# An mLSTM stage on one core: TensorE's order written out with a second branch's products handed out between, and the state weights' exponentials moved

## The chip, the cores and the metric

The kernel runs on one core of a Trainium2 chip. The metric is the device time of one execution in microseconds (us). A core has TensorE (PE: matmuls, with its weight loads shown as PEld), VectorE (DVE), ScalarE (ACT), GpSimd (POOL) and SyncE (SP), which issues most DMAs. Each engine takes its own instructions in order and waits on semaphores for the others.

## What is computed

One decoder layer for 512 tokens of width 1024 in float32: an mLSTM branch and a sliding-window attention branch read the same normalised input, their outputs are gated, merged and projected; then come an MLP, a gated embedding and a last norm. The change touches the mLSTM and the merge:

```
def step(carry, chunk):                       # per head, chunk after chunk
    C, n, m = carry
    b = cumsum(fc); log_d = where(causal, b[t] - b[s] + ic[s], -inf); inter = b + m
    m_t = maximum(inter, max(log_d))
    scores = (q @ k.T) * exp(log_d - m_t)
    w_inter = exp(inter - m_t)
    num = w_inter * (C @ q) + scores @ v
    den = w_inter * (n @ q) + sum(scores)
    h = num / maximum(abs(den), exp(-m_t))
    w = exp(b_last - b + ic - m_new); decay = exp(b_last + m - m_new)
    C_new = decay * C + (w * v) @ k.T;  n_new = decay * n + w @ k
...
y_a = sigmoid(o_ml) * rmsnorm(h) * g
merged = sigmoid(g_a) * (y_a @ w_branch_a) + sigmoid(g_b) * (y_b @ w_branch_b)
```

`y_b` is the output of the attention branch. There are 4 mLSTM heads with keys of width 128 and values of width 256; the kernel uses chunks of 128 tokens, so a sequence has 4 chunks (`NT`) and a head 3 states that are needed.

## The kernel before, in words

Every large product is done in float32 split into two parts (a high part `wh`, made by a cast on ScalarE, and a rest `wl`, by a subtraction on VectorE), three matmuls for each pair of tiles: a 128x128 weight against 512 columns. A projection of one 128-row tile of the output is thus 8 x 3 = 24 matmuls (24 "products"), accumulated in one bank. `load_w` loads a weight tile and splits it; there are four buffers each for the raw tile, the high part and the rest.

Accumulation banks: two of tag `g` (`psg`, one bank each), two of tag `t` (`pst`, one bank each) and two of tag `a` (`psa`, two banks each). Activations of 512 columns (`act_f`, `act_r`) come from one pool of 36 buffers. Two buffers of tag `pT` hold, in the mLSTM stage, pairs of gates read back from DRAM (`gl`). Four buffers of tag `vs` hold the weighted keys `kw`, four of tag `lm` the values.

A tile framework orders the instructions when the kernel is built: a planner goes by program order as the priority and by durations of its own, puts each instruction in as soon as its inputs and a buffer are ready in its plan, and adds the waits. Inside a block `tc.manual_schedule(engines=...)`, the named engines keep the program's order. `tc.issue_after(x)` puts all instructions of its block that run on the engine of `x` behind `x` on that engine.

The stages that matter here:

- First phase (0 to about 60 us), all engines but POOL in manual order: norm, first projections, the projection for the output gates `o` (`o_open` makes the products, `o_close` returns a function that applies the sigmoid, line 264, and stores the gate in DRAM through POOL's queue), and the scans of the mLSTM's forget and input gates on 4 partitions. `mst` is the running maximum; `pk` collects what is transposed later into `gc`: rows 0 to 3 hold exp(-mst), 32 to 35 the exponents `gg`, 64 to 67 the exponents of the states' weights, 96 to 99 those of the inter-chunk weights. The gates' sigmoids are put behind `em_last`, the last exponential of the phase. The rows 96 to 99 go to DRAM as `rid`.
- Value projections, branch gates (`gbd`, `gad` in DRAM), then the sliding-window attention (212 to 324 us) with TensorE in manual order: there the products of other projections are handed out by a generator, `more(n)` emitting the next `n`.
- The mLSTM stage, where the planner orders everything. Per head `h`: `ml_weights` loads the rows `pr` and `pi` (broadcast `rid`), transposes three key chunks (L914) and makes the score products (L916) in one `psa` tile, splits the weighted keys `kw` (L143, L144), forms the decay matrix with exponentials of `dg` (L924, L925), and scales the queries (L928); `ml_state` makes three state products and folds them up (L942, L946); `ml_out` makes the output of four chunks in `pst` banks, copies it to `hs` (L959), takes the denominators (L960 to L965) and sums squares (L968); `ml_norm` scales it. `branch_b(i)` is the projection of `y_b` (24 products), multiplied with a branch gate (`gb`, L986); there are eight. `ya_of(h)` transposes a head's output (L998), multiplies it with the output gate (`sy`, L999) and splits it into `ya`. Then eight projections of `ya` (`w_a`) follow.

Of the kernel before, what the change touches and what calls it, by code (L numbers as in the profile page):

```python
# [23 lines left out]
NH = 4  # L24
# [12 lines left out]
def block_kernel(  # L37
# [49 lines left out]
    def nm(s):  # L87
        n_names[0] += 1
        return f"{s}_{n_names[0]}"


    def ps_g():
        return pp.tile([P, 512], F32, tag="g", bufs=2, name=nm("psg"))

    def ps_t():
        return pp.tile([P, 512], F32, tag="t", bufs=2, name=nm("pst"))
# [9 lines left out]
    def act_f(n="f"):  # L106
        return ap.tile([P, 512], F32, tag="act", bufs=NACT, name=nm(n))
# [28 lines left out]
    def split(dst, src, scale=None):  # L136

        if scale is None:
            done = A.copy(dst[0], src)  # L139
            V.tensor_sub(dst[1], src, r32(dst[0]))  # L140
            return done.ins
        else:
            A.activation(dst[0], src, AF.Copy, scale=scale)  # L143
            V.scalar_tensor_tensor(dst[1], src, scale, r32(dst[0]), ALU.mult, ALU.subtract)  # L144
# [7 lines left out]
    def load_w(src, n, dims, raw=None):  # L152

        if raw is None:
            raw = load_raw(src, n)
        parts = [wp.tile([P, 1024], F32R, tag=t, bufs=WB, name=nm(t))[:, :n] for t in ("wh", "wl")]
        split(parts, raw[:, :n])
        return [q.rearrange("p (k c) -> p k c", k=dims) for q in parts]
# [7 lines left out]
    def chain(ps, ops, first, last, parts=False):  # L166
        for i, (l, r) in enumerate(ops):
            last_mm[0] = T.matmul(ps, l, r, start=first and i == 0, stop=last and i == len(ops) - 1, skip_group_check=parts)  # L168
# [13 lines left out]
    def mm_T(ps, w, acts, first=True, last=True):  # L182

        ops = []
        for k in range(len(acts)):
            ops += pairs([q[:, k, :] for q in w], acts[k])
        chain(ps, ops, first, last)
# [120 lines left out]
    with tc.manual_schedule(engines={ENG.PE, ENG.Activation, ENG.DVE, ENG.SP}):  # L308
# [181 lines left out]
        G.memset(pk, 0.0)  # L490
        mst = act_f("mst")[:4, :]
        V.tensor_tensor_scan(mst, lf, ig, 0.0, ALU.add, ALU.max)
        fl = act_f("fl")[:4, :]
        for c in range(NT):
            V.tensor_tensor_scan(fl[:, c * P : (c + 1) * P], lf[:, c * P : (c + 1) * P], zeros4, 0.0, ALU.add, ALU.add)
# [5 lines left out]
        ends = lambda t: chunks(t)[:, :, P - 1 :].broadcast_to([4, 3, P])  # L501
        V.tensor_tensor(chunks(pk[64:68, :]), chunks(gg), ends(rr), ALU.add)
        V.tensor_tensor(chunks(pk[96:100, :]), chunks(rr[:, P:]), ends(mst), ALU.add)
        A.activation(pk[:4, :], mst, AF.Exp, scale=-1.0)
        em_last = A.activation(pk[64:100, : 3 * P], pk[64:100, : 3 * P], AF.Exp).ins
        V.tensor_copy(pk[32:36, :], gg)
        for i in (3, 4):
            gates.append(o_close(i, o_open(i, hT, ow[i])))
# [206 lines left out]
    def gate_of(put, i):  # L715

        if i % 2 == 0:
            loaded[0] = sp.tile([P, 2, 512], F32, tag="pT", bufs=2, name=nm("gl"))
            nc.sync.dma_start(out=loaded[0], in_=put[i // 2])
        return loaded[0][:, i % 2, :]  # L720

    gbd = gate_proj(w_gb)
    gad = gate_proj(w_ga)
# [159 lines left out]
    def h_of(h, t):  # L883
        return hs[h][t // 2][:, (t % 2) * DV : (t % 2 + 1) * DV]

    def ml_weights(h):
        pr = sp.tile([P, 512], F32, tag="pr", bufs=2, name=nm("pr"))
        nc.sync.dma_start(out=pr, in_=rrd[h : h + 1, :].broadcast_to([P, 512]))
        pi = act_f("pi")[:, : 3 * P]
        nc.sync.dma_start(out=pi, in_=rid[h : h + 1, :].broadcast_to([P, 3 * P]))  # L890
        dg = act_f("dg")
        V.tensor_tensor(
            dg.rearrange("p (t j) -> p t j", t=NT),
            pr.rearrange("p (t j) -> p t j", t=NT),
            tri.unsqueeze(1).broadcast_to([P, NT, P]),
            ALU.add,
        )
        if h < 2:
            room = bp.tile([P, KT, 512], F32R, tag="big", bufs=2, name=nm("wT"))
            wT = [room[:, k, :] for k in range(2)]  # L900
            qw = [room[:, k, : 3 * P] for k in range(2, 4)]
            rest = room[:, 4:, :].rearrange("p k c -> p (k c)")
            cs = [[rest[:, (2 * c + j) * (DV + 2) : (2 * c + j + 1) * (DV + 2)] for j in range(2)] for c in range(3)]
        else:
            wT, qw = act_hl("wT"), [t[:, : 3 * P] for t in act_hl("qw")]
            cs = None
        vhl = [head_values() for _ in range(2)]
        for s in range(NT):
            split([v[:, s, :] for v in vhl], vm[s][:, h, :])
        both = ps_a()  # L910
        kt, psc = both[:, 512:], both[:, :512]
        block = lambda t, s: t[:, s * P : (s + 1) * P]
        for s in range(3):
            T.transpose(block(kt, s), block(qk[4 + h], s), ident)  # L914
        for s in range(NT):
            T.matmul(block(psc, s), block(qk[4 + h], s), block(qk[h], s), start=True, stop=True)  # L916
        kw = []
        for s in range(3):
            t = sp.tile([P, 2 * P], F32R, tag="vs", bufs=4, name=nm("kw"))
            kw.append([t[:, :P], t[:, P:]])  # L920
            split(kw[s], block(kt, s), gc[:, 2 * NT + s, h : h + 1])
        dm = act_f("dm")
        for s in range(NT):
            A.activation(block(dm, s), block(dg, s), AF.Exp, bias=gc[:, s, h : h + 1])  # L924
        V.tensor_mul(dm, psc, dm)  # L925
        split(wT, dm)
        qt = act_f("qt")[:, : 3 * P]
        V.tensor_mul(qt, qk[h][:, P:], pi)  # L928
        split(qw, qt)
        wts[h] = wT, qw, cs, kw, vhl, pi  # L930

    def ml_state(h):
        wT, qw, cs, kw, vhl, pi = wts[h]
        if cs is None:
            t = [sp.tile([P, 2 * (DV + 2)], F32R, tag="cs", bufs=3, name=nm("cs")) for _ in range(3)]
            cs = [[c[:, : DV + 2], c[:, DV + 2 :]] for c in t]
        two = ps_a()
        ps = [t[:, : DV + 2] for t in (two[:, :512], two[:, 512:], ps_t())]
        for s in range(3):
            chain(ps[s], pairs(kw[s], [v[:, s, :] for v in vhl]), True, True)  # L940
        state = act_f("st")[:, : DV + 2]
        A.copy(state, ps[0])  # L942
        split(cs[0], state)
        for s in range(1, 3):
            new = act_f("st")[:, : DV + 2]
            V.scalar_tensor_tensor(new, state, pi[:, s * P - 1 : s * P], ps[s], ALU.mult, ALU.add)  # L946
            state = new
            split(cs[s], state)
        wts[h] = wT, qw, cs, vhl

    def ml_out(h):
        wT, qw, cs, vhl = wts.pop(h)
        for t in range(NT):
            pn = ps_t()
            ops = pairs([w[:, t * P : (t + 1) * P] for w in wT], [v[:, t, :] for v in vhl])
            if t:
                ops += pairs([q[:, (t - 1) * P : t * P] for q in qw], cs[t - 1])
            chain(pn[:, : DV + 2], ops, True, True)
            A.copy(h_of(h, t), pn[:, :DV])  # L959
            V.tensor_copy(hd[:, h, t : t + 1], pn[:, DV : DV + 1])  # L960
        den = small("den", NT, 2)
        V.scalar_tensor_tensor(den, hd[:, h, :], -1.0, hd[:, h, :], ALU.mult, ALU.max)
        V.tensor_max(den, den, gc[:, NT : 2 * NT, h])
        rd = small("rd", NT, 3)
        V.reciprocal(rd, den)  # L965
        jk = act_f("jk")
        for t in range(NT):
            A.activation(jk[:, :DV], h_of(h, t), AF.Square, scale=rd[:, t : t + 1], accum_out=hss[:, h, t : t + 1])  # L968
        return rd
# [9 lines left out]

    t2 = [None] * 8  # L980

    def branch_b(i):
        ps = ps_g()
        mm_T(ps, load_w(w_b[i], KT * P, KT), yb)
        t2[i] = act_f("gb")
        V.tensor_mul(t2[i], ps, gate_of(gbd, i))  # L986


    ya = []

    def ya_of(h):
        if not ya:
            ya.extend(big_hl("ya")[1])
        for i in (2 * h, 2 * h + 1):
            sg = act_f("sy")
            pt = ps_t()
            for t in range(NT):
                T.transpose(pt[:, t * P : (t + 1) * P], h_of(h, t)[:, (i % 2) * P : (i % 2 + 1) * P], ident)  # L998
            V.scalar_tensor_tensor(sg, pt, gml[:, i : i + 1], gate_of(god, i), ALU.mult, ALU.mult)  # L999
            split(ya[i], sg)  # L1000

    ml_weights(0)
    ml_state(0)
    rds = []
    for h in range(NH):
        branch_b(2 * h)
        if h + 1 < NH:
            ml_weights(h + 1)
        if h < 2:
            ml_state(h + 1)  # L1010
        rds.append(ml_out(h))
        if h == 2:
            ml_state(h + 1)
        branch_b(2 * h + 1)
        if h == 1:
            ml_norm([0, 1], rds)
        elif h > 1:
            ml_norm([h], rds[h:])
            ya_of(h - 2)
    ya_of(2)  # L1020
    ya_of(3)


    mg = []
# [403 lines left out]
```

## Time and profile before

| | |
|---|---|
| median of 3 runs | 887.67 us (886.52 to 888.81) |
| the profiled execution | 886.76 us, span from first to last instruction 884.4 us |
| TensorE | busy 870.4 us, 98% of the span |
| VectorE, ScalarE | busy 655.2 us (74%), 452.1 us (51%) |
| granted TensorE clock | 0.998 on the mean |
| mLSTM stage, 324.1 to 404.4 us | VectorE busy 63.69 us, ScalarE 57.20 us |

How to read the lines of the profile. A group reads: line, engine, operation, output tile <- input tiles, shape, count, busy us, mean ns of one, idle time of the engine before them and what ended it. A wait reads: engine, tile and line that waited <- what it waited for: us in total, times, longest. A row of the timeline reads: start, duration, engine, line, operation, tiles, shape, count, and in brackets the idle time before it. A row of a stretch reads: from:to, us, then the busy time of PE, PEld, DVE, ACT (and POOL) with the number of instructions, the granted clock, the share of DMA time and GB/s. Where instructions were picked by tile or line, such a row counts only those. Ends of matmuls are modelled, so a busy TensorE may still lose time.

### The profile page before, as it was taken

The page shows a single profiled execution, that of the slowest core. Times are in us where ns is not written, and L with a number is a line of the kernel's source. Part 1 is how long each engine was busy: PE and PEld are TensorE (multiplying, and loading weights), DVE is VectorE, ACT ScalarE, POOL GpSimd, SP SyncE. Part 2 cuts the span into 40 slices and gives each one's busy share as a digit, 9 for nine tenths or more (in the row PEclk, how much of TensorE's full clock was granted, in tenths as well). Part 3 has the DMA queues.
Part 4 walks back from the last instruction along what each step waited for, and adds up shares of the span by engine and source line. Part 5 has one row for each costly group of instructions (what it writes and reads, how often), then busy time and mean ns, then how long its engine had stood idle before and what let it go on. Part 6 is the DMA issues. An engine that isn't in the chain of part 4 may idle for free.

```text
span 884.4 us, 11952 instructions
## 1 busy us (share of the span) xinstructions
PE 870.4 (98%) x4588; PEld 731.9 (83%) x4588; DVE 655.2 (74%) x1057; ACT 452.1 (51%) x753; POOL 13.1 (1%) x36
## 2 busy tenths in 40 slices
PE   9999999999999999999999999999999999999996
PEld 8878899998877877878888888888888888888886
DVE  5998787864887888678534679767957885798556
ACT  6564444454666677764323645335434533444844
POOL 1010000000000000000000000000000000000000
PEclk9999999999999999999999999999999999999999
DMA  8651324453121133336352611620352054102402
GB/s 337 214 203 58 122 96 144 152 172 130 49 72 59 61 129 113 104 104 206 123 186 85 225 48 61 201 96 24 120 176 85 1 190 143 49 24 76 138 1 96
DMA packets 31289, 103.37 MB, mean 117 GB/s; under 512 B 4344, under 2 KB 5372, under 8 KB 31232
## 3 DMA queue, kind: packets, MB, share of 16 engines
q1 hardware_dynamic: 29232, 96.04, 32.0%
q0 software_dynamic: 1856, 6.31, 2.0%
q8 instruction: 36, 0.59, 0.3%
q10 hardware_dynamic: 144, 0.26, 0.1%
q14 instruction: 21, 0.17, 0.1%
HBM read 94.19 MB, written 8.40 MB: 116 GB/s over the span
## 4 chain that ended last, share of the span: by engine, by line
PE 89%; DVE 2%; ACT 1%; issue 0%; ACTq 0%; DVEq 0%
PE psg L168 42%; PE psp L168 23%; PE psa L168 9%; PE psg L844 8%; PE pst L819 2%; PE psa L772 1%; PE psa L806 1%; PE pst L168 1%; PE psp L1058 1%; PE psa L916 0%; DVE prod L1262 0%; PE pst L998 0%; DVE it L1283 0%; ACT sgp L1269 0%; ACT z L1297 0%
## 5 line engine op out<-in xcount | busy, mean ns | idle before, releaser
L139 ACT CAST wh<-wr 128x1024 fp32r<-128x1024 f32 x128 | 134.3, 1051 | 195.0 <-PE psg L168 69.2
L140 DVE TENSOR_TENSOR wl<-wr,wh 128x1024 fp32r<-128x1024 f32 x128 | 155.9, 1221 | 89.5 <-ACT wh L139 89.5
L168 PE MATMUL psg<-x,wh 128*128 128x512 f32 x512 | 158.3, 390 | 0.0
L168 PE MATMUL psp<-wh,uf 128*128 128x512 f32 x448 | 139.1, 390 | 0.0
L168 PEld LDWEIGHTS psg<-x,wh 128*128 128x128 f32 x512 | 96.1, 188 | 19.8
L168 PE MATMUL psg<-x,wl 128*128 128x512 f32 x256 | 99.7, 389 | 0.0
L168 PEld LDWEIGHTS psp<-wh,uf 128*128 128x128 f32 x448 | 84.1, 188 | 17.3
L168 PE MATMUL psp<-wl,uf 128*128 128x512 f32 x224 | 87.3, 390 | 0.0
L139 ACT CAST wh<-wd 128x1024 fp32r<-128x1024 f32 x44 | 46.3, 1055 | 57.7 <-PE psp L168 26.0
L844 PE MATMUL psg<-h,wh 128*128 128x512 f32 x192 | 62.4, 400 | 0.0
L140 DVE TENSOR_TENSOR wl<-wd,wh 128x1024 fp32r<-128x1024 f32 x44 | 53.5, 1220 | 4.4 <-ACT wh L139 4.1
L168 PEld LDWEIGHTS psg<-x,wl 128*128 128x128 f32 x256 | 48.1, 188 | 9.9
L168 PE MATMUL psa<-h,wh 128*128 128x256 f32 (+1 forms) x240 | 50.2, 306 | 1.3 <-ACT sgo L264 1.3
L168 PEld LDWEIGHTS psp<-wl,uf 128*128 128x128 f32 x224 | 42.1, 188 | 8.7
L140 DVE TENSOR_TENSOR uf<-F,uf 128x1792 fp32r<-128x1792 f32 (+2 forms) x20 | 33.0, 1651 | 21.8 <-ACT uf L139 21.8
L168 PEld LDWEIGHTS psa<-h,wh 128*128 128x128 f32 x240 | 38.8, 191 | 4.3 <-ACT sgo L264 1.7
L844 PEld LDWEIGHTS psg<-h,wh 128*128 128x128 f32 x192 | 35.4, 188 | 8.2 <-issue 0.4
L168 PE MATMUL psg<-yb,wh 128*128 128x512 f32 x128 | 41.4, 396 | 0.6 <-DVE gb L986 0.6
L139 ACT CAST uf<-F 128x1792 fp32r<-128x1792 f32 (+2 forms) x20 | 28.0, 1398 | 26.3 <-DVE F L1134 26.2
L1120 DVE SCALAR_TENSOR_TENSOR rt<-psg,rB 128x512 f32<-128x512 f32 x32 | 22.1, 689 | 25.6 <-PE psg L168 25.6
L168 PE MATMUL psg<-ya,wh 128*128 128x512 f32 x128 | 40.5, 395 | 0.0
L791 ACT ACTIVATE lm<-lm,nmx 128x256 f32<-128x256 f32 (+1 forms) x64 | 30.0, 470 | 17.2 <-DVE nmx L784 15.6
(329 smaller groups left out, 1747.3 us busy)
## 6 DMA issues: line engine op xcount, KB each, us to landing
wr<-in_w_up SPq DMA_DIRECT2D x32, 512.0 KB, 3.3
wd<-in_w_down SPq DMA_DIRECT2D x24, 512.0 KB, 3.4
wr<-in_w_o SPq DMA_DIRECT2D x8, 512.0 KB, 6.9
gd<-gr POOLq DMA_DIRECT2D x8, 512.0 KB, 3.0
wr<-in_w_qsw SPq DMA_DIRECT2D x8, 512.0 KB, 3.6
wr<-in_w_qkml SPq DMA_DIRECT2D x8, 512.0 KB, 3.8
wr<-in_w_b SPq DMA_DIRECT2D x8, 512.0 KB, 3.3
gl<-gd SPq DMA_DIRECT2D x8, 512.0 KB, 3.4
```

Of the source, the lines that this page charges most:

```text
L139: done = A.copy(dst[0], src)
L140: V.tensor_sub(dst[1], src, r32(dst[0]))
L168: last_mm[0] = T.matmul(ps, l, r, start=first and i == 0, stop=last and i == len(ops) - 1, skip_group_check=parts)
L772: T.matmul(o, q[x][HALF[ab], n * P : (n + 1) * P], keys[kp][y][HALF[ab], k0 : k0 + 256], start=i == 0, stop=i == 2)
L791: A.activation(lm3[:, g, :], lm3[:, g, :], AF.Exp, bias=nmx[:, g : g + 1], accum_out=sm[:, g : g + 1])
L806: T.transpose(pt[:, c : c + P], lm3[:, g, j * P : (j + 1) * P], ident)
L819: T.matmul(o[HALF[ab], m * 256 : (m + 1) * 256], vs[n + m + 1 - nk + j][:, c : c + 64], pTs[m][:, j * 512 + ab * 256 : j * 512 + (ab + 1) ...
L844: T.matmul(ps, l, r, start=k == 0 and j == 0, stop=k == KT - 1 and j == 2)
L1058: T.transpose(ps[:, m * P : (m + 1) * P], xk[m][:, k * P : (k + 1) * P], ident)
L1120: V.scalar_tensor_tensor(a, ps, 0.0, rB, ALU.max, ALU.mult)
```

## The change

Three things are changed. In the first phase the exponential of `-mst` moves right behind the scan that makes `mst` and becomes the one that the gates' sigmoids are put behind; the second exponential of the phase, over 36 partitions of `pk`, is gone. In its place, the mLSTM stage applies an exponential to 12 columns of `gc` once, and one to `pi` in each `ml_weights`. The whole stage runs with TensorE in manual order: the eight projections of branch b become a generator from which `more(n)` takes products between the parts of the heads, `ya_of` becomes `ya_tile` for one of eight tiles, and two groups of products are handed out inside each `ml_out`. Gates in use are kept by source, so that branch gates and output gates can be in use side by side.

```diff
+        em_last = A.activation(pk[:4, :], mst, AF.Exp, scale=-1.0).ins     # behind the scan of mst
...
-        A.activation(pk[:4, :], mst, AF.Exp, scale=-1.0)
-        em_last = A.activation(pk[64:100, : 3 * P], pk[64:100, : 3 * P], AF.Exp).ins
...
         if i % 2 == 0:
-            loaded[0] = sp.tile([P, 2, 512], F32, tag="pT", bufs=2, name=nm("gl"))
-            nc.sync.dma_start(out=loaded[0], in_=put[i // 2])
-        return loaded[0][:, i % 2, :]
+            loaded[id(put)] = sp.tile([P, 2, 512], F32, tag="pT", bufs=2, name=nm("gl"))
+            nc.sync.dma_start(out=loaded[id(put)], in_=put[i // 2])
+        return loaded[id(put)][:, i % 2, :]
...
         nc.sync.dma_start(out=pi, in_=rid[h : h + 1, :].broadcast_to([P, 3 * P]))
+        A.activation(pi, pi, AF.Exp)
...
             chain(pn[:, : DV + 2], ops, True, True)
+            if t in (1, 2):
+                more(7 - 2 * t)
...
-    def branch_b(i):
-        ps = ps_g()
-        mm_T(ps, load_w(w_b[i], KT * P, KT), yb)
+    def b_done(i, ps):
         t2[i] = act_f("gb")
         V.tensor_mul(t2[i], ps, gate_of(gbd, i))
...
-    ml_weights(0)
-    ml_state(0)
     rds = []
-    for h in range(NH):
-        branch_b(2 * h)
-        if h + 1 < NH:
-            ml_weights(h + 1)
-        if h < 2:
-            ml_state(h + 1)
-        rds.append(ml_out(h))
-        if h == 2:
-            ml_state(h + 1)
-        branch_b(2 * h + 1)
-        if h == 1:
-            ml_norm([0, 1], rds)
-        elif h > 1:
-            ml_norm([h], rds[h:])
-            ya_of(h - 2)
-    ya_of(2)
-    ya_of(3)
+    A.activation(gc[:, 2 * NT :, :], gc[:, 2 * NT :, :], AF.Exp)
...
+    def branches():
+        for i in range(8):
+            w = load_w(w_b[i], KT * P, KT)
+            ps = ps_g()
+            for k in range(KT):
+                for j, (l, r) in enumerate(pairs([t[:, k, :] for t in w], yb[k])):
+                    T.matmul(ps, l, r, start=k == 0 and j == 0, stop=k == KT - 1 and j == 2)
+                    yield
+            b_done(i, ps)
+        yield
+
+    fill = branches()
+
+    with tc.manual_schedule(engines={mybir.EngineType.PE}):
+        more(24)
+        ml_weights(0)
+        ml_weights(1)
+        more(24)
+        ml_state(0)
+        ml_state(1)
+        more(20)
+        rds.append(ml_out(0))
+        ml_weights(2)
+        more(17)
+        rds.append(ml_out(1))
+        ml_state(2)
+        ml_weights(3)
+        norm_of([0, 1])
+        more(17)
+        rds.append(ml_out(2))
+        ml_state(3)
+        norm_of([2])
+        for i in range(4):
+            more(4)
+            ya_tile(i)
+        rds.append(ml_out(3))
+        norm_of([3])
+        more(21)
+        ya_tile(4)
+        more(5)
+        ya_tile(5)
+        more(15)
+        ya_tile(6)
+        for _ in fill:
+            pass
+        ya_tile(7)
```

More of the change, by code (lines that the diff above doesn't have):

```diff
@@ L989, in block_kernel, with ya_tile @@
     ya = []
-    def ya_of(h):
+    def ya_tile(i):
+        h = i // 2
         if not ya:
             ya.extend(big_hl("ya")[1])
[L994 to L1000, printed above, removed]
-    ml_weights(0)
@@ L1003, in block_kernel @@
-    ml_state(0)
-    rds = []
-    for h in range(NH):
-        branch_b(2 * h)
-        if h + 1 < NH:
-            ml_weights(h + 1)
-        if h < 2:
-            ml_state(h + 1)
-        rds.append(ml_out(h))
-        if h == 2:
-            ml_state(h + 1)
-        branch_b(2 * h + 1)
-        if h == 1:
-            ml_norm([0, 1], rds)
-        elif h > 1:
-            ml_norm([h], rds[h:])
-            ya_of(h - 2)
-    ya_of(2)
-    ya_of(3)
+        sg = act_f("sy")
+        pt = ps_t()
@@ new lines, in ya_tile, with norm_of @@
+        for t in range(NT):
+            T.transpose(pt[:, t * P : (t + 1) * P], h_of(h, t)[:, (i % 2) * P : (i % 2 + 1) * P], ident)
+        V.scalar_tensor_tensor(sg, pt, gml[:, i : i + 1], gate_of(god, i), ALU.mult, ALU.mult)
+        split(ya[i], sg)
+    rds = []
+    A.activation(gc[:, 2 * NT :, :], gc[:, 2 * NT :, :], AF.Exp)
+    def norm_of(heads):
+        ml_norm(heads, [rds[h] for h in heads])
+    def branches():
[8 more added lines that the diff above has]
+        yield
```

## The prediction

> **What bounds the kernel now.** I read the page's busy times first, then TensorE's waits, then the timeline around the one wait of the early phase, and last the mLSTM stage (324 to 404 us) alone.
>
> ```profile
> PE 870.4 (98%) x4588; PEld 731.9 (83%) x4588; DVE 655.2 (74%) x1057; ACT 452.1 (51%) x753; POOL 13.1 (1%) x36
> PE pst L998 <- DVE st L946: 1.4, 1, 1.4
> PE psa L168 <- ACT sgo L264: 1.3, 1, 1.3
> ```
>
> TensorE bounds it, and the waits listed for it are short; these are the longest, the first in the mLSTM stage, the second in the early phase. A matmul's end is modelled, though, so short stalls hide in "busy". For the stage I therefore compare the time elapsed with the work done at the undisturbed pace. First the counts: the 512-wide products into `psg`; all matmuls of line 168; then the transposes of L998, the score matmuls of L916 and the transposes of L914.
>
> ```profile
> 324.10:404.40 80.30, 56.67 (x221) 39.40 (x221) 7.58 (x11) 0.00 (x0) 1.00 0.38 128
> 324.10:404.40 80.30, 71.07 (x341) 54.63 (x341) 1.00 0.38 128
> 324.10:404.40 80.30, 4.83 (x32) 3.92 (x32) 1.00 0.38 128
> 324.10:404.40 80.30, 4.23 (x32) 3.88 (x32) 1.00 0.38 128
> 324.10:404.40 80.30, 1.96 (x12) 1.53 (x12) 1.00 0.38 128
> ```
>
> Then the pace, from stretches of the chain of waits in which TensorE ran on without a stop (start, us, what, count):
>
> ```profile
> 347.27 1.43 PE pst L168 x12
> 337.63 0.89 PE psa L916 x8
> 373.93 7.30 PE psg L168 x32
> 395.46 0.88 PE pst L998 x8
> ```
>
> So a product costs 7.30/32 = 0.228 us, a 258-wide matmul 0.119, a score matmul or transpose 0.11. The work is 221 x 0.228 + (341 - 221) x 0.119 + 76 x 0.11 = 50.4 + 14.3 + 8.4 = 73.1 us in 80.3 us: **7.2 us are lost in the stage**. The waits of the weight loads say where:
>
> ```profile
> PEld psa L168 <- ACT kw L143: 2.1, 5, 0.7
> PEld pst L998 <- DVE st L946: 1.8, 1, 1.8
> PEld psa L168 <- DVE kw L144: 1.1, 3, 0.6
> PEld psg L168 <- DVE gb L986: 1.0, 2, 0.5
> ```
>
> The state products come up before their weighted keys `kw` are split (339 to 341.5 and 350 to 354 us), and at 384.5 us the gated output's transposes wait for a bank that the state's update has not read yet. All three are matters of order, none of total load: VectorE is busy 63.7 and ScalarE 57.2 of these 80.3 us.
>
> **The change part by part.**
>
> *1. Exponential of `mst` early, the second one (L505) out of the first phase.* TensorE and ScalarE around the early wait:
>
> ```profile
> 56.69 0.61 PE L168 MATMUL psa<-h,wh 128*128 128x512 f32 x2
> 57.14 0.39 PE L168 MATMUL psa<-h,wl 128*128 128x512 f32 x1
> 58.83 0.73 PE L168 MATMUL psa<-h,wh 128*128 128x512 f32 x2 [1.30 <-ACT sgo L264]
> 50.58 0.63 ACT L504 ACTIVATE pk<-mst 4x512 f32<-4x512 f32 x1 [2.31 <-DVE mst L492]
> 51.90 1.06 ACT L139 CAST wh<-wr 128x1024 fp32r<-128x1024 f32 x1 [0.69 <-PE psa L168]
> 54.78 0.52 ACT L505 ACTIVATE pk<-pk 36x384 f32<-36x384 f32 x1 [1.83 <-DVE pk L503]
> 55.32 1.28 ACT L264 ACT_TABLE_LOAD   x1
> 56.62 1.67 ACT L264 ACTIVATE sgo<-sgo 128x512 f32<-128x512 f32 x3
> 58.20 0.57 ACT L264 ACTIVATE sgo<-psa 128x512 f32<-128x512 f32 x1
> ```
>
> The gates' sigmoids are tied behind the last exponential, which waits for VectorE until 54.78. TensorE's next output projection waits for the fourth sigmoid (58.77). With the exponential of `mst` (done at 51.21) as the last one, table load, three sigmoids, the cast of 51.90 and the fourth sigmoid take 1.28 + 1.67 + 1.06 + 0.57 = 4.6 us, to about 55.8, ahead of TensorE's 57.4. The gap from 57.14 to 58.83 is 1.69 instead of the usual 0.23: **-1.46 us** (none at worst, if the planner puts the sigmoids later). The work up to 324 us has nothing that would hold this back: the DMA of `rid` on POOL leaves a little earlier, and the next weights are cast ahead.
>
> The three small state weights now go through a 12-column exponential, traced before the stage but ready at 71 us, so the planner may place it between two sigmoids, at the price of two table loads, 2 x 1.28 us. ScalarE waits for TensorE there:
>
> ```profile
> 69.83 1.05 ACT L139 CAST wh<-wr 128x1024 fp32r<-128x1024 f32 x1 [3.33 <-PE psg L168]
> 75.74 1.05 ACT L139 CAST wh<-wr 128x1024 fp32r<-128x1024 f32 x1 [4.36 <-PE psg L168]
> ```
>
> 4.36 us of idle time covers 2.6: I cost it at nothing; without that cover it would be at most 2.6. The Trainium skill ("ScalarE: Activation LUTs", What ACT_TABLE_LOAD costs) adds a drain of about 1.38 us to each load, 2.66 in all; by it the two switches would need 5.3 us and overrun the gap by 1. The trace disagrees: the sigmoid at 56.62 starts 0.02 us after its load ends.
>
> *2. Exponential of `pi` (128x384) in each `ml_weights`.* ScalarE does a 384-wide cast in this time:
>
> ```profile
> L139 ACT CAST qw<-qt 128x384 fp32r<-128x384 f32 x2 | 1.0, 514 | 3.1 <-DVE qt L928 3.1
> 325.12 0.42 SPq L890 DMA_DIRECT2D pi<-rid  x1
> DMA to landing us min/median/max: 3.4/3.8/6.4
> 332.26 1.28 ACT L924 ACT_TABLE_LOAD   x1
> 328.31 3.69 DVE L756 SCALAR_TENSOR_TENSOR acc<-acc,sg 128x512 f32<-128x512 f32 x6
> ```
>
> 4 x 0.51 = 2.1 us on ScalarE, off the path. Behind the first one queue the exponentials of the decay; it waits for `pi` to land, 331.5 at the latest (325.12 + 6.4), before the table load has ended (333.54). So no new wait.
>
> *3. TensorE in program order, products of branch b in between.* The ideal is that all 7.2 us go. Counting on from 324.1 in the new order: 24 products to 329.6; keys and scores of heads 0 and 1 (2 x 11 x 0.11 = 2.4) to 332.0; 24 products to 337.5; state 0 (9 x 0.119) to 338.5; then state 1. Two places are late next.
>
> *State 1.* The three splits `kw` of a head use four buffers in all, so the second and third of head 1 wait until state 0 has read the first two of head 0, and state 1 needs the bank in which head 1's keys and scores lie.
>
> ```profile
> L143 ACT ACTIVATE kw<-psa,gc 128x128 fp32r<-128x128 f32 x12 | 4.3, 359 | 1.4 <-PE psa L916 1.2
> L144 DVE SCALAR_TENSOR_TENSOR kw<-psa,gc,kw 128x128 fp32r<-128x128 f32 x12 | 4.2, 346 | 1.1 <-ACT kw L143 1.1
> 324.00:332.00 8.00, 8.00 (x43) 6.59 (x42) 7.96 (x15) 7.05 (x13) 0.00 (x0) 1.00 0.65 221
> 332.00:340.00 8.00, 7.72 (x43) 6.21 (x42) 6.94 (x15) 6.95 (x16) 0.00 (x0) 1.00 0.37 123
> ```
>
> The second product group of state 0 ends at 338.2 (6 x 0.119); split on ScalarE 0.36, on VectorE 0.35, handover 0.2: 339.1 against 338.5, a stall of at least 0.6. VectorE and ScalarE are nearly full in these 16 us (VectorE gets free of the silu only at 332.0), so up to 2.5. I take **+1.5**.
>
> *The gates of the first four `ya` tiles.* The tag `pT` has two buffers. When the `ya` tiles come, one holds the branch gates 4 and 5 until product 144 is done, which stands behind them in the order (at 142). So the output gates 2 and 3 load into the other buffer only after `ya` tile 1 is multiplied, and the two `pst` banks stay taken until tiles 2 and 3 are multiplied, while head 3's output needs them.
>
> ```profile
> DMA to landing us min/median/max: 3.1/3.7/5.5
> L999 DVE SCALAR_TENSOR_TENSOR sy<-pst,gml,gl 128x512 f32<-128x512 f32 x7 | 5.0, 745 | 0.0
> ```
>
> After tile 1's transposes: multiply 0.85, load 3.5, multiply 0.85 = 5.2 us; TensorE has 8 products and 8 transposes meanwhile, 2.7. Stall 2.5, and 0.1 for the restart: **+2.6** (2.1 with the fastest load; 4.0 with a queue ahead on VectorE).
>
> *Restarts and small waits.* The 58.83 row shows two matmuls in 0.73 where others take 0.61: 0.12 a restart. In each head's output 5 products (1.1 us) cover the release of the first bank, which a 1.22 us split ahead on VectorE can overrun. I take **+0.8** (0.3 to 1.5).
>
> All else has cover: each state's chain (a copy, two updates, three splits) gets 16 to 20 products and more before its head's output (3.6 to 4.6 us), and the last `ya` tile is due 23 products later in branch a's first tile.
>
> The sum: -1.46 - 7.2 + 1.5 + 2.6 + 0.8 = **-3.8 us**. The profiled execution took 886.76 us (span 884.4, 2.4 around it), 0.9 below the median of 887.67; against the median, 887.67 - 3.8 = 883.9. With the low ends of the three unknowns (0.6 + 2.1 + 0.3 = 3.0 for 4.9) it is 882.0, and up to 885.0 I count as this case.
>
> **The rivals.**
>
> *A, the new waits are as long as the old.* State 1 stalls 2.5, the gates 4.0, the rest 1.5: 8.0 against 7.2. Only the early phase is left: -0.7, 887.0. For it speaks the full VectorE from 324 to 340; against it that VectorE has 16.6 us free in the stage.
>
> *B, slower: the activation buffers run out at the `ya` tiles.* Of 36, then live: `yb` 16, heads 6, gated products 5, `wT` and `qw` of head 3 4, states 3, `pi` 1 = 35. With one left, each tile waits until the one before is multiplied and split.
>
> ```profile
> L139 ACT CAST ya<-sy 128x512 fp32r<-128x512 f32 x7 | 4.2, 612 | 3.3 <-DVE sy L999 3.2
> L140 DVE TENSOR_TENSOR ya<-sy,ya 128x512 fp32r<-128x512 f32 x6 | 4.0, 682 | 0.0
> ```
>
> 0.75 + 0.61 + 0.68 and queues make 3 us a tile: from the end of state 3, tile 0 at 4.5 (when the state's chain gives a buffer back, an estimate), then 7.5, 11.9 (gate load) and 14.9, and head 3's output stalls 9.9 instead of 2.6. +7.3: 891.2. It decides if no buffer of the state chain is back when tile 1 comes; against it, the three states and `pi` come free as soon as that chain is split. A stall this long bears on the clock too: every window above shows 1.00 granted. The Trainium skill ("TensorE: Matmul & The Clock Gate", HAM oscillation) says that an idle gap above about 3.4 us drops the clock to half; by it B would lose some 1.7 us more (an estimate from that page), and the forecast's 2.6 us nothing. No run here shows such a gap.
>
> *C, the gate wait does not come*, because the second gate load finds a buffer early: -3.8 - 2.6 = -6.4, 881.3. Against it stands the order of the products in the code.
>
> *D, the early edit does nothing*, since the planner places the sigmoids as late as before: 885.4.
>
> **How the numbers follow.** Forecast 0.40, A 0.22, B 0.14, C 0.17, D 0.07. What a measurement of this kernel can tell from no change is about 0.3%, 2.7 us. Faster by more: forecast and C, 0.57; within: A and D, 0.29; slower: B, 0.14. The range goes from C with some of its unknowns at their low ends, 880.5, over A to part of the way to B, 889.0.
>
> **What would show it.** Part 1: no wait of `psa` on L264, and the sigmoid table loaded near 52 us. Part 3: no `pst` L998 wait on L946, no `kw` waits near 351; instead a wait of state 1 on `kw` or `dm` near 337 and one of head 3's first output on the multiply of `ya` tile 2, some 45 us later. The products and transposes keep their pace. The prediction is wrong if ScalarE's or VectorE's order, made by a planner with its own durations, puts a late-needed step ahead of `kw`, or if the stalls move to places not named here.

## The result: 16 us slower, and the profile after

The changed kernel takes 903.67 us (median of 4 runs, 903.28 to 903.88) against 888.11 for the kernel before beside it: a ratio of 1.0177 [1.0160, 1.0195]. The forecast was 883.9. The profiled execution has a span of 901.3 us (before 884.4) at a mean granted clock of 0.987.

In the changed kernel L1014 are the products of branch b, L961 and L962 the copies of an output chunk (`hs` on ScalarE, `hd` on VectorE; both must be done before its bank is free), L925 the multiply of the scores with the decay, L999 the multiply of a `ya` tile. TensorE's waits:

```profile
PE pst L168 <- DVE hd L962: 8.4, 2, 4.4
PE psa L168 <- DVE dm L925: 3.5, 1, 3.5
PE pst L168 <- DVE sy L999: 2.6, 1, 2.6
PE psg L168 <- DVE ya L140: 0.7, 1, 0.7
```

Five waits, all for VectorE: at 337 us (state 1), at 360 and 377 (third chunk of the outputs of heads 1 and 2), at 393 (head 3's output) and at 418. Between the starts of the matmuls around them 3.7, 4.2, 4.5, 2.8 and 1.0 us are missing, 16.2 in all. The stage's products, up to the 220th, in the form of the row of before:

```profile
323.00:421.20 98.20, 59.24 (x220) 42.43 (x221) 7.71 (x11) 0.00 (x0) 0.90 0.36 113
```

By the prediction's pace the same work needs 220 x 0.228 + 120 x 0.119 + 76 x 0.11 = 72.8 us: 25.4 us are lost where 7.2 were before. The 16.2 us of standing still explain two thirds. The rest is in the granted clock, which was 1.00 throughout the stage before. It changes only at the ends of stretches of 3.41 us (last section). Such stretches around the first two waits and around the one at 393 (PE busy, PEld, DVE, ACT, POOL, then the clock):

```profile
335.71:339.13 3.42, 2.01 (x14) 1.62 (x12) 2.52 (x7) 3.19 (x9) 0.00 (x0) 1.00 0.52 143
339.13:342.54 3.41, 1.31 (x10) 1.34 (x11) 3.41 (x7) 1.68 (x4) 0.00 (x0) 1.00 0.36 113
342.54:345.95 3.41, 3.41 (x9) 2.64 (x9) 3.31 (x9) 2.02 (x6) 0.00 (x0) 0.50 0.12 46
345.95:349.37 3.42, 3.42 (x19) 2.92 (x19) 0.59 (x2) 0.37 (x2) 0.00 (x0) 1.00 0.44 153
359.61:363.02 3.41, 0.82 (x4) 0.35 (x2) 2.49 (x4) 1.57 (x2) 0.00 (x0) 1.00 0.00 0
363.02:366.43 3.41, 1.92 (x8) 1.86 (x9) 1.43 (x5) 1.31 (x4) 0.00 (x0) 0.50 0.64 178
366.43:369.85 3.42, 3.42 (x16) 3.23 (x15) 1.59 (x7) 1.82 (x6) 0.00 (x0) 0.50 0.50 187
393.74:397.15 3.41, 1.34 (x9) 1.13 (x10) 2.66 (x6) 1.33 (x3) 0.00 (x0) 1.00 0.16 65
397.15:400.57 3.42, 3.42 (x14) 2.94 (x13) 2.60 (x5) 1.60 (x3) 0.00 (x0) 0.50 0.61 184
```

Behind the first wait (from 342.54) TensorE is busy, at half clock: 9 matmuls in 3.41 us where 15 products would fit. Six such slow stretches (342.5, 363.0 and 366.4, 380.1 and 383.5, 397.2; two behind each of the waits of 4.2 and 4.5 us) make 20.5 us; TensorE is busy for 17.0 of them, and up to half of that, 8.5 us, is lost. With the restarts behind the waits that makes up the other 9 us.

The first phase did what was forecast. The sigmoid table loads at 51.48 instead of 55.32, no matmul waits for L264, and branch b starts at 323.0 instead of 324.1:

```profile
50.84 0.63 ACT L493 ACTIVATE pk<-mst 4x512 f32<-4x512 f32 x1 [2.31 <-DVE mst L492]
51.48 1.28 ACT L264 ACT_TABLE_LOAD   x1
...
70.05 1.28 ACT L1003 ACT_TABLE_LOAD   x1
71.48 0.21 ACT L1003 ACTIVATE gc<-gc 128x12 f32<-128x12 f32 x1 [0.16 <-DVE gc L587]
74.43 1.05 ACT L139 CAST wh<-wr 128x1024 fp32r<-128x1024 f32 x1 [2.73 <-PE psg L168]
75.50 1.28 ACT L264 ACT_TABLE_LOAD   x1
```

The 12-column exponential does fall between two sigmoids with two table loads, and idle time of ScalarE covers them, as costed.

**What ends the long waits.** The wait at 360 us, on TensorE, ScalarE and VectorE in turn:

```profile
359.82 0.61 PE L1014 MATMUL psg<-yb,wh 128*128 128x512 f32 x2
364.51 0.77 PE L168 MATMUL pst<-vh,wT 128*128 128x258 f32 x2 [4.08 <-DVE hd L962]
```

```profile
359.78 1.05 ACT L139 CAST wh<-wr 128x1024 fp32r<-128x1024 f32 x1 [0.56 <-PE psg L1014]
360.74 0.61 ACT L139 CAST wT<-dm 128x512 fp32r<-128x512 f32 x1
363.19 0.51 ACT L139 CAST qw<-qt 128x384 fp32r<-128x384 f32 x1 [1.84 <-DVE qt L928]
363.61 0.64 ACT L961 COPY hs<-pst 128x256 f32<-128x256 f32 x2
```

```profile
360.86 1.23 DVE L140 TENSOR_TENSOR wl<-wr,wh 128x1024 fp32r<-128x1024 f32 x1 [0.92 <-ACT wh L139]
362.00 0.69 DVE L140 TENSOR_TENSOR wT<-dm,wT 128x512 fp32r<-128x512 f32 x1
362.61 0.55 DVE L928 TENSOR_TENSOR qt<-acc,pi 128x384 f32<-128x384 f32 x1
363.74 0.56 DVE L140 TENSOR_TENSOR qw<-qt,qw 128x384 fp32r<-128x384 f32 x1 [0.58 <-ACT qw L139]
364.21 0.15 DVE L962 COPY hd<-pst 128x1 f32<-128x1 f32 x1
```

The first chunk was ready before 359. Its copy (`hs`, 0.37 us) stands on ScalarE behind the cast of weights for later and two splits of head 2, whose output starts only at 375; one of them waits 1.84 us for VectorE, where the subtraction of the same weights (1.23 us) stands ahead. Both engines are idle for part of this stretch (2.49 and 1.57 us busy of 3.41, above): they have time, but not the right instruction in front. At 377 us the picture is the same, with a table load for the norm's square root and the norm's eight scalings in the queues.

### The profile page after: what moved, and what is told of

It reads as the page before. It is cut to its first block, busy times and chain, and to the rows that moved or that the text cites. A ratio compares the mean times of both kernels' runs of the same rounds, so it can differ in the third digit from the quotient of the medians.

```text
span 901.3 us, 11959 instructions
## 1 busy us (share of the span) xinstructions
PE 876.2 (97%) x4588; PEld 739.1 (82%) x4588; DVE 655.9 (73%) x1057; ACT 453.6 (50%) x757; POOL 13.2 (1%) x36
## 4 chain that ended last, share of the span: by engine, by line
PE 76%; DVE 4%; ACT 3%; DMA 1%; issue 1%; ACTq 0%; DVEq 0%
PE psg L168 32%; PE psp L168 23%; PE psg L843 7%; PE psa L168 4%; PE psg L1014 3%; PE pst L168 2%; PE pst L818 1%; PE psa L771 1%; PE psa L805 1%; DMA gl<-god 1%; PE psp L1090 1%; ACT jk L970 1%; DVE sy L999 0%; ACT dm L924 0%; DVE hs L979 0%
## 5 line engine op out<-in xcount | busy, mean ns | idle before, releaser
L1014 PE MATMUL psg<-yb,wh 128*128 128x512 f32 x128 | 43.8, 419 | 0.0
```

The lines of the kernel that those rows point to most:

```text
L1014: T.matmul(ps, l, r, start=k == 0 and j == 0, stop=k == KT - 1 and j == 2)
```

## The experiments

Ratios are to the kernel before on the same chip. **Theory**: the fixed order of TensorE makes it wait for one instruction after another that the planner, with durations of its own, has put deep into ScalarE's and VectorE's queues, and each long wait also costs clock. **Rivals**: too few buffers; too much work for the two engines; the moved exponentials.

**1. The exponentials alone**, in the kernel before:

```diff
+        em_last = A.activation(pk[:4, :], mst, AF.Exp, scale=-1.0).ins   # behind the scan
-        A.activation(pk[:4, :], mst, AF.Exp, scale=-1.0)
-        em_last = A.activation(pk[64:100, : 3 * P], ...).ins
+        A.activation(pi, pi, AF.Exp)                      # in ml_weights
+    A.activation(gc[:, 2 * NT :, :], gc[:, 2 * NT :, :], AF.Exp)
```

> The kernel before with the moved exponentials alone (the early one, the one on the states' weights, the one on pi); TensorE's order in the mLSTM stage is the planner's. If the early edit does what its wait said and the stage's loss is all from the new order: the wait of psa on L264 is gone and the time falls by 1.1 to 1.5 us, to 886.6 to 887.0. If the exponentials of pi on ScalarE delay the stage: 888 or more, with new waits on kw or wT there.

885.55 us (883.76 to 886.14), 0.9974 [0.9964, 0.9984]: 2.0 us faster. In this order of the stage the exponentials cost nothing; the loss comes with the other part of the change.

**2. The change without the fixed order** (`with tc.manual_schedule(engines={PE}):` becomes `if True:`).

> The changed kernel without the manual block: the same program order as priority, the same products handed out, but the planner may place TensorE's matmuls. Theory (TensorE stands still because its order is fixed while ScalarE's and VectorE's is the planner's): TensorE fills the waits and the time is 884 to 891. Rival (the new order of the heads itself asks too much of ScalarE, VectorE and the buffers): 897 or more, with the same long stalls.

889.75 us (888.05 to 891.09), 1.0015 [1.0002, 1.0028]. Against experiment 1 the changed kernel loses 18 us: 14 of them come with TensorE's fixed order, and the other 4 with the new sequence of the heads under the planner, which has three waits of 1.9, 2.0 and 2.9 us, for `kw`, `hd` and `sy`, and three slow stretches.

**3. Six buffers for the key splits** (`tag="vs", bufs=4` becomes 6).

> The changed kernel with six buffers for the weighted keys instead of four. If the buffers make state 1 late: its stall of 3.7 us falls to 0.7 to 1.5 and the stretch at half clock behind it (1.7 us) goes: 899 to 900. If VectorE is simply full there: the stall stays above 2.5 and the time at 902 to 904.

903.15 us (900.81 to 903.59), 1.0169 [1.0153, 1.0186]: no change, and state 1 still waits 3.9 us. Buffers are not what it waits for. (In a further run, the kernel of experiment 1 with six key buffers took 885.29 us against its 885.55: no change there either.) VectorE's queue in the changed kernel shows what is:

```profile
337.67 0.56 DVE L928 TENSOR_TENSOR qt<-acc,pi 128x384 f32<-128x384 f32 x1 [0.90 <-ACT pi L890]
...
338.41 0.68 DVE L986 TENSOR_TENSOR gb<-psg,gl 128x512 f32<-128x512 f32 x1
339.01 1.22 DVE L140 TENSOR_TENSOR wl<-wr,wh 128x1024 fp32r<-128x1024 f32 x1
340.14 0.35 DVE L144 SCALAR_TENSOR_TENSOR kw<-psa,gc,kw 128x128 fp32r<-128x128 f32 x1
340.40 0.68 DVE L925 TENSOR_TENSOR dm<-psa,dm 128x512 f32<-128x512 f32 x1
```

The last row frees the bank. Its input was ready at 337.2; ahead of it stand the scaled queries, which wait 0.90 us for the new exponential of `pi`, a branch product and a weight split, all due later. The 0.90 us is part of the wait of state 1.

**4. Three buffers for the gates** (tag `pT`, with 35 activation buffers instead of 36).

> The changed kernel with three buffers of tag pT instead of two (and 35 activation buffers instead of 36, for the space). If the second load of output gates holds up head 3's output: its stall of 2.8 us, the 1.0 us in the first tile of branch a and one stretch at half clock (1.7 us) go: 898 to 899. If something else released those waits: 903 to 904.

902.29 us (900.40 to 903.46), 1.0163 [1.0145, 1.0181]: 1.4 us of the expected 5, and the interval overlaps that of the changed kernel. The gate's load did end the wait at 393: in the changed kernel it is issued only when the buffer is free,

```profile
391.55 0.32 SPq L718 DMA_DIRECT2D gl<-god  x1
```

and L999 waits for it until 394.97. But it ends that wait by only 0.72 us: until 394.26 VectorE is busy with splits and the four scalings of head 2's norm, which stand ahead of L999. So with three buffers the wait falls from 2.6 to 1.7 and no further. The one at 418 goes, 0.7 comes in at 389, and the one at 377 grows to 5.1.

**5. The products inside the outputs of heads 1 and 2** (`more(17)` ahead becomes `more(2)`, `more(5)` within becomes `more(20)`).

> For heads 1 and 2, fifteen of the products that stood ahead of the head's output are handed out between its second and third chunk instead. Theory: the release of the first bank comes as late as before, but TensorE has 15 x 0.228 = 3.4 us more to do meanwhile, so the stalls at 360 and 377 us fall from 4.2 and 4.5 to about 1, and the two slow stretches behind them (13.6 us at half clock together) go; against it, state 2's chain has lost 3.4 us of its cover ahead of output 2, worth up to 3 us there. Together 892 to 898. Rival (the two engines' throughput sets the pace, so the stall moves to the next thing that TensorE needs): 901 to 904.

903.67 us (900.39 to 904.59), 1.0164 [1.0140, 1.0187]: a miss, both waits are as long as before (4.1 and 4.0 us). My expectation was built wrongly: what TensorE waits for is the end of a queue that starts when head 2's scores are made. From the start of the scores to the copy of the first chunk it is 10.4 us in both kernels (353.24 to 363.61, here 354.79 to 365.16), and between those scores and the third chunk stand 22 products in either version. Cover counts from where the queue starts, not from the chunk.

**6. TensorE kept busy ahead of state 1** (the third product group of state 0 made ten times over).

> The third product group of state 0 is repeated ten times (30 matmuls in all, same result), so that TensorE works for about 3.2 us of the 3.7 that it stood still ahead of state 1. The end of that wait stays where it is. Theory (standing still is what halves the clock behind it): the slow stretch of 342.5 to 346 us is gone, 8 products at 0.227 instead of 0.427 us, so 1.6 us less: about 902. Rival (the clock falls for another reason): the slow stretch stays, 903.7 or up to 1 us more.

900.77 us (899.81 to 901.44), 1.0143 [1.0128, 1.0158]: 2.9 us less, though the wait's end has not moved (state 1 starts at 341.45, in the changed kernel at 341.23).

```profile
337.40 3.70 PE L168 MATMUL pst<-vh,kw 128*128 128x258 f32 x30
341.45 0.95 PE L168 MATMUL psa<-vh,kw 128*128 128x258 f32 x6 [0.34 <-DVE dm L925]
```

```profile
343.50:347.00 3.50, 3.50 (x17) 2.85 (x16) 3.26 (x9) 1.76 (x6) 0.00 (x0) 1.00 0.02 5
```

27 needless matmuls make the kernel faster: the slow stretch behind the wait is gone. It is standing still that costs the clock. The 2.9 us are more than this one stretch, priced at 1.6: in this execution the wait from 359 to 363 also has one slow stretch behind it instead of two, since it falls differently on the stretches of 3.41 us.

**7. All three engines ordered by hand**, a first attempt.

> TensorE's order is that of the changed kernel, instruction for instruction, through the whole stage; ScalarE and VectorE are put in a fixed order too, in which what releases a bank for TensorE's next product stands ahead of work that is due later (copies of an output behind its matmuls, squares and exponentials for later heads after them, weights split two projections ahead, the second half of the silu products behind the first states). The key splits have six buffers. Theory (the stalls come from where the releasing instructions stand in the two queues): the stalls at 337, 360 and 377 us fall from 3.7, 4.2 and 4.5 to under 1.5 each, no stretch at half clock is left behind them, and the time is 881 to 889. Rival (VectorE or ScalarE has too much to do for this order of TensorE, whatever its own order): stalls of 3 us and more stay or appear elsewhere, with their slow stretches, and the time stays above 895.

905.85 us (905.63 to 905.97), 1.0200 [1.0186, 1.0214]: a miss, and for the moment the rival had the better of it. The trace shows the faults of my order: at 358 us four squares of head 0 stand ahead of the copies of head 1 (3.2 us), at 378 the squares and the table load ahead of the norm (3.3), at 401 the multiply of a branch product behind a weight's split, a norm and two `ya` splits (2.8). And the key splits of a head take turns, which I had not allowed for:

```profile
ACT kw L143 <- DVE kw L144: 2.5, 4, 0.9
```

ScalarE starts the next split only when VectorE has read the bank for the last one. The Trainium skill ("PSUM — Partial Sum Buffer", PSUM bank collisions raise a hardware error) says that two engines must not be in one bank at once, reads included, and that the compiler's scheduler puts a dependency between them. The trace agrees: the two engines take turns here, with 2.5 us in four waits.

**8. All three engines in order of need.** The same order of TensorE; the two queues come from a list made with the durations of the traces, each engine taking what is due first among what is ready. A part of it (suffix A: on ScalarE, D: on VectorE; `o_mm` makes a chunk of an output, `hsA` and `hdD` copy it, `wTA` is a split of head 2, `sq` a square of head 0):

```diff
+        o_mm(1, 0)
+        kwD(2, 2)
+        dmD(2)
+        o_mm(1, 1)
+        hsA(1, 0)
+        vD(2, 3)
+        more(1)
+        wTA(2)
+        hdD(1, 0)
...
+        sq(0, 2)
```

> TensorE's order is again that of the changed kernel, instruction for instruction. ScalarE and VectorE are put, instruction by instruction, in the order in which TensorE needs their results (a list made from the durations in the traces, in which each engine always takes what is due first among what is ready); unlike the first attempt by hand, no square, silu product or split for a later head stands ahead of a copy that frees a bank, and other work stands between the three key splits of a head, which take turns on the two engines. Theory (the stalls come from the order of the two queues): no stall over 1.2 us is left in the stage, no stretch at half clock, the stage loses 3 to 7 us in all where the changed kernel lost 24, and the time is 882 to 887. Rival (the two engines have too much to do for this order of TensorE): stalls of 2 us and more stay, with slow stretches behind them, and the time is 893 or more.

880.55 us (879.51 to 881.74), 0.9919 [0.9906, 0.9933]: 23 us faster than the changed kernel with the same order of TensorE, and faster than both kernels. The copies of head 1, on ScalarE, and TensorE's longest waits in the stage:

```profile
353.17 0.35 ACT L1034 COPY hs<-pst 128x256 f32<-128x256 f32 x1
353.42 0.62 ACT L973 CAST wT<-dm 128x512 fp32r<-128x512 f32 x1
353.94 0.37 ACT L1034 COPY hs<-pst 128x256 f32<-128x256 f32 x1
354.27 1.05 ACT L1136 CAST wh<-wr 128x1024 fp32r<-128x1024 f32 x1
```

```profile
PE pst L168 <- DVE sy L1102: 0.7, 1, 0.7
PE pst L168 <- DVE st L1012: 0.4, 1, 0.4
```

No stretch of the stage is at half clock, and the 221 products and what goes with them take 76.1 us: 3.0 are lost. VectorE is busy for 70.2 and ScalarE for 62.2 of these 76.1 us, so the rival of too much work is refuted. Output gates are loaded ahead of branch gates here, four silu products come later, and six key buffers and weights split further ahead belong to it. What each of these is worth in this order was not run alone; more buffers gained at most 1.4 us in the changed kernel (experiments 3 and 4), and experiment 11 tests the order by itself at one place.

**9. As 8, with the products dealt out anew** among the same parts.

> As the kernel with the queues in order of need, with the products of branch b dealt out anew among the same parts of the heads (one to seven between two chunks of an output instead of five and three, four between the first two heads' scores, and so on). If the order of the queues is what matters, this is within 1.5 us of that kernel, 881 to 887; if cover by products inside the outputs is, it is more than 3 us faster than that kernel.

881.18 us (880.83 to 882.19), 0.9927 [0.9915, 0.9940]: within 0.7 us of experiment 8. (The list of the two queues is made anew for it.) Where exactly the products stand matters little once the queues are right.

**10. One edit of the changed kernel**: head 2's and 3's late splits behind the copies.

```diff
+    def ml_back(h):                       # wT, qt, qw of heads 2 and 3
+        with tc.issue_after(last_copy[0].ins), tc.issue_after(last_copy[1].ins):
+            backs[h]()
...
         rds.append(ml_out(1))
+        ml_back(2)
```

> The changed kernel with one edit: for heads 2 and 3, the splits of the score weights and the scaled queries with theirs (3.4 us on VectorE, 2.2 on ScalarE for both heads) are put behind the copies of the output before them. TensorE's order is the same. Theory: the copy that frees the bank at 360 us no longer stands behind the cast of the next weights and these splits, so that stall falls from 4.2 to under 1 us and the slow stretch behind it goes; at 377 us the table load, the weights' cast and the norm's scaling still stand ahead, so that the stall falls from 4.5 to about 3 and its slow stretch stays. Stalls at 337 and 393 us stay. Together 3.3 + 1.5 of waits and up to 3.4 of slow clock: 896 to 899. Rival (throughput): what is put off comes due at the next output, the waits only move, and it stays at 902 to 905.

900.22 us (898.96 to 900.42), 1.0140 [1.0125, 1.0155]: 3.4 us faster, short of what was expected.

```profile
PE pst L1012 <- DVE st L960: 3.7, 1, 3.7
PE pst L168 <- DVE hd L976: 3.3, 1, 3.3
PE pst L168 <- DVE sy L1013: 2.3, 1, 2.3
```

The wait at 360 is gone, as expected; state 1 still waits 3.5 us. But the planner now takes the norm's root earlier, so that head 3's exponentials need their table again (1.28 us at 371.0) and the copy at 371 is late; and head 3's splits, put off, stand with a norm's root and its table load ahead of its state's update (first row). This is half of what the rival said: put off without a due time, work comes in the way of something else.

**11. One fault put back into experiment 8**: ahead of head 1's first two copies stand one split of head 2, a weight's cast and four squares.

```diff
-        hsA(1, 0)
...
+        fin(0)
+        wTA(2)
         wA(7)
...
+        for t in range(NT):
+            sq(0, t)
+        hsA(1, 0)
+        hdD(1, 0)
```

> The kernel with the queues in order of need (880.55), with one fault of the changed kernel put back: on ScalarE, the split of head 2's score weights, the cast of the next weights and the four squares of head 0 stand ahead of head 1's first two output copies again. Nothing else is moved by more than its place in that group, and TensorE's order is the same. Theory: the first copy comes about 4 us later (0.6 + 1.05 + 2.5), TensorE stands still for 2.7 to 3.5 us at 354.8, and the stretch behind it runs at half clock for about 3.4 us, which costs another 1.5: 884.5 to 886. If a stall has no effect on the clock, 883.2 to 884; if the queue's order does not matter there, 880.5.

886.30 us (883.57 to 888.35), 0.9989 [0.9976, 1.0003]: 5.7 us slower than experiment 8 (6.2 by the ratios). The wait is 3.3 us, and a slow stretch follows:

```profile
352.80:356.22 3.42, 2.20 (x14) 1.64 (x12) 2.37 (x6) 2.98 (x7) 0.00 (x0) 1.00 0.14 19
356.22:359.63 3.41, 1.33 (x9) 1.24 (x10) 0.92 (x3) 2.35 (x9) 0.00 (x0) 1.00 0.34 135
359.63:363.04 3.41, 3.41 (x17) 3.32 (x15) 2.78 (x8) 0.62 (x3) 0.00 (x0) 0.50 0.27 68
```

So 3.5 between the starts of the matmuls for the wait and about 1.6 for the clock, both from the order of the queues at one place. Another 0.7 us is a wait for a DMA late in the kernel. The scatter of these runs goes with the clock: the two shortest, 883.57 and 884.04 us, have a mean granted clock of 0.998, and the four longest, 887.60 to 888.35, have 0.993 or 0.994. The two shortest lie about where the expectation put a wait without effect on the clock. Only one execution was traced, so that the wait falls differently on the stretches in each is likely but not shown.

## Why the prediction was wrong

The forecast left 4.9 us of losses in the stage; 25.4 came. State 1 took 3.7 of them (forecast 1.5), the gates 2.8 (2.6), restarts and small waits 9.7 (0.8), and 9.2 are the clock and the restarts behind the waits (nothing for the clock). The steps in turn:

- *Part 1, -1.46.* Right: no wait for L264. The stage starts 1.1 us earlier, and with the other exponentials the edit gained 2.0 us alone (experiment 1).
- *The 12-column exponential at nothing.* Right, at the place and with the cover that were named.
- *The exponential of `pi` at nothing.* Right in the kernel before's order (experiment 1). In the changed one VectorE waits 0.90 us for it ahead of the instruction that ends the wait of state 1. The step checked that the first `pi` is in time for ScalarE, not what waits behind the exponential on VectorE.
- *The stage's 7.2 us go.* The old waits for `kw` and for L946 did go. The step that failed stands next to it: "All else has cover". Cover was counted in products against the length of one chain, as if the chain's instructions started when their inputs were ready. They start when the queue gets to them.
- *State 1, +1.5.* It came where it was placed, at 3.7 us instead of 1.5 (beyond the bound of 2.5), and for another reason: not four buffers (experiment 3), but the queue in front of L925. The prediction had named `dm` as one of two things that state 1 could wait for, but its lower figure counted the `kw` splits alone, and nothing counted what stands ahead of `dm` on VectorE.
- *The gates, +2.6.* It came, at 2.6 (2.8 with the restart), and the load named ended it. That the size fits is luck in part: VectorE's queue alone would have held TensorE for most of it, and with a third buffer 1.7 us remain (experiment 4).
- *Restarts and small waits, +0.8.* This is the term that broke. It said that 5 products cover the release of the first bank, which one 1.22 us split could overrun; two of the outputs waited 4.2 and 4.5 us, since a weight's cast, splits of the next head and, at 377, a root and eight scalings stood ahead; 1.0 more came at 418. The instruction that frees a bank had to wait for its turn, and no number of products behind the scores was counted against that.
- *The clock.* The forecast counted none; up to 8.5 us came. Rival B had priced it for a 9.9 us wait only, and for "the forecast's 2.6 us nothing", by the Trainium skill's rule on idle gaps above 3.4 us. The trace disagrees: behind the gates' wait of 2.6 us the stretch from 397.15 is at half clock (first table of stretches).

The last sentence of the prediction named the cause, a planner's order that "puts a late-needed step ahead", as what would make it wrong, and gave it no price. The trace of before would have given one: there ScalarE already does squares, exponentials, two splits and a weight's cast between head 2's scores (349.9) and the next output copies (361.7). No rival contained it; A stopped at 8.0 us of waits, and B named activation buffers, to which none of the waits above was traced.

## What to carry to other kernels

Fixing the order of one engine makes its partners' queues part of the path: before an order is written out, list for each wait what stands ahead of the releasing instruction on its engine, and put the releases (copies out of a bank) ahead of work that is due later. If one engine's order is fixed by hand, fix the others' by due time as well: the same TensorE order cost 16 us with the planner's queues and gained almost 8 with ordered ones and what belongs to experiment 8, 2 of them from the exponentials. Price a wait of TensorE at its length and, where it leaves TensorE idle for more than about half of a stretch of 3.41 us, at up to some 1.6 us more for each slow stretch behind it; here there were one or two.

## What the runs showed of the hardware

In these traces the granted clock is decided stretch by stretch, on a grid of 3.41 us, by how busy TensorE was in the stretch before. In the changed kernel it changes at 342.54, 345.95, 363.02, 369.85, 380.09, 386.91, 397.15 and 400.57, all whole multiples of 3.413 us apart. There 2.01 us busy left the next stretch at 1.00, and 1.31 and 0.82 put it at 0.50 (rows above). In experiment 7 a wait of 3.2 us at 358 was split by the grid, and the clock stayed:

```profile
356.50:359.92 3.42, 1.72 (x10) 1.16 (x8) 1.40 (x3) 2.93 (x11) 0.00 (x0) 1.00 0.44 169
359.92:363.33 3.41, 1.91 (x13) 1.78 (x14) 1.86 (x7) 2.79 (x10) 0.00 (x0) 1.00 0.00 0
363.33:366.74 3.41, 3.41 (x29) 3.28 (x28) 3.00 (x10) 2.41 (x7) 0.00 (x0) 1.00 0.00 0
```

In experiment 2 a wait of 1.9 us fell into one stretch, and the clock was halved:

```profile
336.06:339.47 3.41, 1.53 (x10) 1.18 (x9) 2.60 (x5) 3.07 (x7) 0.00 (x0) 1.00 0.22 58
339.47:342.89 3.42, 3.42 (x12) 2.85 (x11) 3.32 (x8) 1.03 (x2) 0.00 (x0) 0.50 0.49 153
```

So what counts is not the length of a wait but whether it leaves a stretch busy for less than about half: 1.72 and 1.88 us (experiment 7, 336 us) left the clock alone, 1.53 and 1.76 (experiment 7, 418 us) did not, and with modelled ends the limit can't be told closer. Once slow, 1.92 us busy (363.02 in the changed kernel) did not end it, nor did 2.54 (experiment 5, 340.78); a stretch that was busy throughout did. The grid lies elsewhere in each trace, and with it the price of a wait: in experiment 5 the wait of state 1 (3.8 us) has two slow stretches behind it, 340.8 to 347.6, where the changed kernel's (3.5 us) has one. The Trainium skill ("TensorE: Matmul & The Clock Gate", What's actually happening) describes a free-running window of 3413 ns, with which these stretches agree; its rule against idle gaps above about 3.4 us (HAM oscillation) is too lenient here, as the wait of 1.9 us shows.
